# A hybrid attention and RWKV-7 layer on one core: accumulator banks, early pieces, compression weights, the y transposes and the corner products changed together

## The chip, the core and the metric

The kernel runs on one core of a Trainium2 chip. Its time is device time in microseconds (us) of one execution; several executions were timed, and the median counts. Engines are named as in the profile: PE is the matmul engine TensorE (PEld its weight loads), DVE is VectorE, ACT is ScalarE, POOL is GpSimd, and SP is the queue that issues nearly all DMAs.

## What is computed

One decoder layer over 256 tokens of width 2048, in float32: a pre-norm, one combined input projection, two groups of heads that read its columns, an output projection, a post-norm and the residual.

```
hn = rms_norm(h, pre_norm_g)
proj = hn @ w_in
q, kv6, gates, z_a, feat_b, z_b = split(proj)
o_a = nsa_mixer(q, k_cmp, v_cmp, k_slc, v_slc, k_win, v_win, gates, ...)   # 8 heads of 128
o_b = rwkv7_mixer(feat_b, ...)                                             # 16 heads of 64
mix = concat([o_a * silu(z_a), o_b * silu(z_b)])
h = h + rms_norm(mix @ w_out, post_norm_g)
```

The attention group compresses its keys and values in blocks of 32 tokens (`silu(flat @ w1) @ w2`, w1 of 4096 x 128 for keys and for values). The RWKV group runs a recurrence over the tokens for each head: the state is decayed, gets a rank-one correction and a rank-one update, and is read out as y; y is normalized per head, scaled, and gets a bonus term.

## The kernel before

**Pieces.** All products with w_in and w_out are made from float32r parts: a weight tile is cast to a high part H (ACT, L287) and a low part L (DVE, L288), x likewise (xH, xL), and H·xH + H·xL + L·xH is accumulated. The input projection is cut into feature-major pieces of 128 columns (the list `FM`), each in two halves of 24 matmuls of 128x256 (`half_piece`, L379), so piece 27 consists of the halves 270 and 271, and their tiles are called hf270 and lf270. After piece 36 come the token-major pieces (`token_major`, L1118): two windows w, each of six parts (ht00 to ht05, ht10 to ht15), that give values and gates with tokens on the partitions. The output projection has four column blocks n of eight weight parts j each (ho04 is n = 0, j = 4), 12 matmuls of 128x512 to a part.

**Accumulators.** PSUM has eight banks. Two belong to `ppool`, for pieces; six are `banks`, for everything else (L181, L182). The first four pieces (`N_FIRST`) use two of each kind. The next ones up to `N_EARLY` = 6 (L57, L393) also take theirs from `banks`, since no piece can be evacuated before the row statistics of x are known (`row_statistics`, L433, which ends with a copy into `rbc`, L455). In `token_major` both accumulators of a window come from `ppool` (L1121), and ACT evacuates them (L1138, L1139).

**Chains beside the pieces.** Generators run between pieces: they emit a step, yield an estimated time, and go on when the kernel's own clock (`now`, advanced by each matmul) has passed it. The lanes are the RWKV blocks, `solve` (L713) for each half of the RWKV heads, two lanes for attention heads, `compress` (L924) and the gates. Scratch tiles come from an arena of 51 units. The instructions so emitted have priorities by class (chain before evacuation before RWKV before attention before pieces), and a scheduler that assumes a duration for each instruction lays out the final order of every engine. On the chip each engine keeps that order and waits where an operand is late.

**`solve`.** It sends the 32x32 triangular corners of GR through DRAM (L724, L730), inverts them in 31 steps on DVE (L737, L739), stores the inverses and their transposes (zs, zt, L745, L746), loads them back (L759, L766), makes the off-diagonal corner products on PE (L775, L793), and then runs four chunks: G = GR·VS (+ AR·state), the correction with ZB, the state update, and y (L871, L876), which ACT copies out (L878). After the loop it squares y (L888), sums (L889), takes a root (L892) and a reciprocal, scales y (L894), transposes it by head pairs (L903) and adds it into `mix[1]` (L904). `gate_b` (L1108) applies the gate and splits the result into mixB (L1105, L1106), which the parts j = 4 to 7 of the output projection read. The second half's `solve` starts after the first half's loop is over.

**`compress`.** For keys, then for values, it needs w1 in four loads of 512 KB. It keeps one load ahead (L943, L947), and each load is tied to the last or last but one finished half-piece (`pace`).

Of the kernel before, what the change touches and what calls it, by code (L numbers as in the profile page):

```python
# [14 lines left out]
ALU = mybir.AluOpType  # L15

P = 128
T = 256
# [28 lines left out]
V_MU, V_G, V_W0, V_A0, V_KK, V_KA, V_RK, V_LNW, V_LNB = 0, 25, 41, 49, 57, 65, 73, 81, 89  # L47
# [6 lines left out]

N_FIRST = 4

N_EARLY = 6  # L57

NA = 3

# [10 lines left out]

ZLAT = 1.0
GLAT = 1.5

NL = 2

# [43 lines left out]
def hybrid_block(ctx: ExitStack, tc: tile.TileContext, xT, xtok, wfm, wtm, wout, vecs, gpost, lora, table,  # L120
                 onehot, consts, pos, cw1, cw2, out):
    nc = tc.nc
    PE, DVE, ACT, POOL, SP = nc.tensor, nc.vector, nc.scalar, nc.gpsimd, nc.sync
# [34 lines left out]
    def pace(ins, to=None):  # L158


        tc.add_manual_dep(ins.ins, (to or last[0]).ins.name,
                          mybir.DependencyInfo(mybir.DependencyClass.Sync, mybir.DependencyReason.DATA),
                          reason="pace")

    def transpose(o, i, idn):
        now[0] += 0.11
        PE.transpose(out=o, in_=i, identity=idn)  # L167
# [11 lines left out]
    arena = Pool(lambda a, k: arena_[:, a * T:(a + k) * T], UNITS, now)  # L179
    banks_ = ps.tile([P, 8, 512], F32, name="banks")  # L180
    banks = Pool(lambda a, k: banks_[:, NPP + a, :] if k == 1 else banks_[:, NPP + a:NPP + a + k, :], 8 - NPP, now)  # L181
    ppool = Pool(lambda a, k: banks_[:, a, :], NPP, now)  # L182

    def sb(k=1):
        while arena.find(k) is None:
            yield lambda: arena.find(k) is not None
        return arena.take(k)
# [60 lines left out]
    def pick(pool, k, step_=1):  # L248
        until(lambda: pool.find(k, step_) is not None)
        return pool.take(k, step_)  # L250

    def vcol(base, m):
        return vec[:, base + m:base + m + 1]
# [138 lines left out]
    first = deque(pick(ppool if j < NPP else banks, 1) for j in range(N_FIRST))  # L392
    early = deque(pick(banks, 1) for j in range(N_FIRST, N_EARLY))  # L393
    marks = []
# [24 lines left out]
    ident = cst[:, K_ID:K_ID + P]  # L419
# [73 lines left out]
    mix, asked = [None, None], [False, False]  # L493
# [219 lines left out]
    def solve(hb):  # L713
# [49 lines left out]
        for par in range(2):  # L763
            b0 = 64 * (1 - par)
            for a in range(2):
                SP.dma_start(ZT[b0:b0 + 32, :, a, :], ztv[0, par, :, :, a])  # L766
        yield 9.0
        t2p = yield from bank2()
        t2v = t2p[:, :, 0:T].rearrange("p b (j a s) -> p b j a s", j=4, a=2)
        for i in range(4):  # L770
            for hh in range(2):
                for c in range(4):
                    b0 = 64 * (1 - c % 2)
                    q0 = 64 * (i % 2) + 32
# [12 lines left out]
        for i in range(4):  # L787
            for hh in range(2):
                for c in range(4):
                    q = 2 * (i // 2) + hh  # L790
                    j = 4 * q + c
                    q0 = 64 * (i % 2)
# [11 lines left out]
        ysb = ysbs.ap  # L804
        SB, SC, SBo = None, None, None
        for c in range(4):
# [3 lines left out]
            for i in range(4):  # L810
                q0 = 64 * (i % 2)
# [5 lines left out]
            if c:  # L817
                for i in range(4):
                    q0 = 64 * (i % 2)
# [8 lines left out]
            for i in range(4):  # L828
                q0 = 64 * (i % 2)
                for hh in range(2):  # L830
                    o = (i // 2) * P + 64 * hh
# [62 lines left out]
        DVE.tensor_tensor(ysb.rearrange("p (g v) -> p g v", g=16), ysb.rearrange("p (g v) -> p g v", g=16),  # L894
                          rn[:, :, None].to_broadcast([P, 16, 64]), op=ALU.mult)
        yield 2.0
        for i in range(4):
            m = 4 * hb + i
            q0 = 64 * (i % 2)
            ytp = yield from bank()  # L900
            for c in range(4):
                o = T * c + P * (i // 2)
                transpose(ytp[:, 64 * c:64 * c + 64], ysb[q0:q0 + 64, o:o + P], ident[q0:q0 + 64, q0:q0 + 64])  # L903
            DVE.scalar_tensor_tensor(mix[1][:, m, :], ytp[:, :T], vcol(V_LNW, m), mix[1][:, m, :], op0=ALU.mult,  # L904
                                     op1=ALU.add)
            ytp.free(2.0)
            yield 0.5
        ysbs.free(1.0)
# [12 lines left out]
    ready_kv = {"kc": False, "vc": False, "tm": False}  # L921
    POOL.memset(vcS.bitcast(F32), 0.0)

    def compress(a, nm):  # L924
        if a == 0:
            pace(SP.dma_start(post, pos), marks[-2])
            pace(SP.dma_start(w2t, cw2), marks[-2])
        blks = yield from sb(4)
        blk = blks.ap.rearrange("p (j g i) -> p j g i", j=32, g=2)
        POOL.memset(blk[:, :, :, 15:16], 0.0)  # L930
        src = cT[nm].ap
        for g in range(2):
            w_g = bass.AP(tensor=src.tensor, offset=src.offset + g * T, ap=[src.ap[0], [1, 32], [16, 15]])
            DVE.tensor_tensor(blk[:, :, g, 0:15], w_g, post[:, a, :, None].to_broadcast([P, 32, 15]), op=ALU.add)
        cT[nm].free(2.0)
        yield 1.0
        cps = yield from bank()
        w1n = None
        for hf in range(4):
            w1 = w1n  # L940
            if w1 is None:
                w1 = yield from sb(4)
                pace(SP.dma_start(w1[:], cw1[a, :, 8 * hf:8 * hf + 8, :].rearrange("p j d -> p (j d)")), marks[-2])  # L943
                yield 3.0
            if hf < 3:
                w1n = yield from sb(4)
                pace(SP.dma_start(w1n[:], cw1[a, :, 8 * hf + 8:8 * hf + 16, :].rearrange("p j d -> p (j d)")),  # L947
                     marks[-1])
            for j in range(2):
                for q in range(4):  # L950
                    jj = 4 * j + q
                    mm(cps[32 * q:32 * q + 32, 0:P], blk[:, 8 * hf + jj].rearrange("p g i -> p (g i)"),
                       w1[:, jj * P:jj * P + P], start=hf == 0 and j == 0, stop=hf == 3 and j == 1)
            w1.free(1.0)
            yield 2.0
        blks.free(1.0)
        csb = yield from sb()
        DVE.tensor_copy(csb[:, 0:P], cps[:, 0:P])
        cps.free(1.0)
        yps = yield from bank()  # L960
        mm(yps[:, 0:32], csb[:, 0:P], qsum, start=True, stop=True)
        csb.free(1.0)
        yh = tp.tile([P, 32], F32, tag="yh", name=f"yh{nm}")
        DVE.tensor_scalar(yh, yps[:, 0:32], 0.5, None, op0=ALU.mult)
        yps.free(1.0)
        yt = tp.tile([P, 32], F32, tag="yt", name=f"yt{nm}")
        ACT.activation(yt, yh, AF.Tanh)
        DVE.scalar_tensor_tensor(yh, yt, 1.0, yh, op0=ALU.add, op1=ALU.mult)
        yield 2.0
        ops = yield from bank()  # L970
        if a == 0:
            mm(ops[:, 0:32], w2t[:, a, :], yh, start=True, stop=True)
            for g in range(2):
                ACT.activation(KCH[:, g, 128:144], ops[:, 16 * g:16 * g + 16], AF.Copy)
                DVE.tensor_tensor(KCL[:, g, 128:144], ops[:, 16 * g:16 * g + 16], KCH[:, g, 128:144].bitcast(F32),
                                  op=ALU.subtract)
        else:
            for g in range(2):
                mm(ops[0:16, g * P:(g + 1) * P], yh[:, 16 * g:16 * g + 16], w2t[:, a, :], start=True, stop=True)
            opv = ops[0:16, 0:2 * P].rearrange("p (g d) -> p g d", g=2)  # L980
            ACT.activation(vcS[0:16], opv, AF.Copy)
            ACT.activation(vcS[64:80], opv, AF.Copy)
            DVE.tensor_tensor(vcS[32:48], opv, vcS[0:16].bitcast(F32), op=ALU.subtract)
        ops.free(2.0)
        ready_kv[nm] = True
        yield 0.4
# [131 lines left out]
    def token_major():  # L1118
        VV = N_.VV = pick(arena, 4).ap.rearrange("p (w i t) -> p w i t", w=2, i=2)
        for w in range(2):  # L1120
            pts = [pick(ppool, 1) for i in range(2)]  # L1121
            for hf in range(len(TMK) - 1):
                H, L = take()
                with at("proj"):
                    for part in range(2):
                        for k in range(TMK[hf + 1] - TMK[hf]):
                            kk_ = TMK[hf] + k
                            for i in range(2):
                                xs = slice(i * P, (i + 1) * P)
                                if part == 0:  # L1130
                                    mm(pts[i][:, 0:268], xH[:, kk_, xs], H[:, k, :], start=kk_ == 0, stop=False)
                                    mm(pts[i][:, 0:268], xL[:, kk_, xs], H[:, k, :], start=False, stop=False)
                                else:
                                    mm(pts[i][:, 0:268], xH[:, kk_, xs], L[:, k, :], start=False, stop=kk_ == NK - 1)
                progress()
            with at("evac"):
                for i in range(2):
                    ACT.activation(VV[:, w, i, :], pts[i][:, 0:T], AF.Copy, scale=rst[:, i:i + 1])  # L1138
                    ACT.activation(gate[:, i, 12 * w:12 * w + 12], pts[i][:, T:268], AF.Tanh, scale=rsth[:, i:i + 1])  # L1139
                    pts[i].free(1.0)  # L1140
        DVE.tensor_scalar(gate, gate, 0.5, 0.5, op0=ALU.mult, op1=ALU.add)
        ready_kv["tm"] = True
# [6 lines left out]
    for j, (nm, i) in enumerate(FM):  # L1149
# [27 lines left out]
        elif nm in ("r", "v"):  # L1177
            o = pick(arena, 1)
# [66 lines left out]
    for n in range(NA):  # L1245
        pts = out_part(n, range(4), ppool if n % 2 == 0 else banks)
# [51 lines left out]
    for n in range(4):  # L1298
# [7 lines left out]
        pts = out_part(n, js, ppool if n % 2 == 0 else banks, order)  # L1306
# [85 lines left out]
```

## Time and profile before

| | |
|---|---|
| time, median of 3 runs (lowest to highest) | 577.52 us (576.17 to 577.62) |
| the profiled execution | 575.76 us, of which the program's span is 574.0 us |
| PE busy | 557.3 us (97%), 4812 matmuls |
| PEld busy | 519.4 us |
| DVE busy | 426.7 us (74%) |
| ACT busy | 311.8 us |
| POOL busy | 55.8 us |
| DMA | 99.97 MB, mean 174 GB/s |
| granted TensorE clock, mean over the span | 0.996 of full speed |

Busy time on PE is the union of its matmuls. Idle time of an engine that nothing waits for costs nothing, so the list of what PE waited for is the view to read with it. Times in the trace count from the start of the span.

### The profile page before, as it was taken

How to read it: one execution, taken by the hardware profiler on the slowest of the kernel's cores; microseconds unless marked ns; L12 is line 12 of the kernel's file. 1: busy time of each engine (PE TensorE's matmuls, PEld its weight loads, DVE VectorE, ACT ScalarE, POOL GpSimd, SP SyncE). 2: the span in 40 equal slices, each digit the busy share in tenths (PEclk: the TensorE clock that was granted, in tenths of full speed). 3: DMA queues.
4: the chain of work that ended last, by engine and by line, in shares of the span. 5: the costliest groups of instructions: out<-in, count | busy, mean ns of one | idle time of the engine just before them, and what ended most of it. 6: DMA issues, size and time to landing. Idle time of an engine off the chain costs nothing.

```text
span 574.0 us, 12180 instructions
## 1 busy us (share of the span) xinstructions
PE 557.3 (97%) x4812; PEld 519.4 (90%) x4812; DVE 426.7 (74%) x892; ACT 311.8 (54%) x566; POOL 55.8 (10%) x95
## 2 busy tenths in 40 slices
PE   9999999999999999999999999999999999999994
PEld 8998999998989999999988999999999987777883
DVE  5888997867988666569789369899766473576855
ACT  6858764623445434457675468566633353564632
POOL 3202300400000000141031000000000000000002
PEclk9999999999999999999999999999999999999998
DMA  8967444557675844333346253356634455674723
GB/s 293 367 199 248 148 163 140 189 156 237 215 268 154 214 145 148 121 114 104 99 138 212 95 156 120 120 167 209 186 114 146 136 158 188 185 293 153 227 90 147
DMA packets 41365, 99.97 MB, mean 174 GB/s; under 512 B 14395, under 2 KB 17116, under 8 KB 40924
## 3 DMA queue, kind: packets, MB, share of 16 engines
q1 hardware_dynamic: 41020, 98.88, 53.2%
q8 instruction: 38, 0.62, 0.5%
q10 hardware_dynamic: 288, 0.31, 0.2%
q14 instruction: 19, 0.16, 0.1%
HBM read 93.93 MB, written 5.24 MB: 173 GB/s over the span
## 4 chain that ended last, share of the span: by engine, by line
PE 78%; DMA 7%; DVE 5%; ACT 4%; issue 2%; SPq 1%; POOL 1%; DVEq 0%; ACTq 0%
PE banks L154 76%; PE banks L167 2%; DMA arena<-in_cw_dram 2%; DMA us<-GR 1%; DMA arena<-us 1%; DMA rf__96<-in_wfm_dram 1%; DMA rf__2334<-in_wfm_dram 1%; DMA zs<-arena 1%; DMA arena<-zt 1%; DVE y L1289 0%; SPq L724 0%; DVE small L537 0%; ACT arena L1036 0%; ACT L892 0%; POOL arena L627 0%
## 5 line engine op out<-in xcount | busy, mean ns | idle before, releaser
L154 PE MATMUL banks<-arena 128*32 128x128 f32 (+3 forms) x470 | 32.3, 255 | 2.1 <-POOL arena L269 1.1
L154 PEld LDWEIGHTS banks<-arena 128*32 128x32 f32 (+3 forms) x470 | 26.6, 137 | 5.7 <-DMA arena<-in_cw_dram 1.5
L737 DVE TENSOR_TENSOR arena<-arena 64x31 f32<-64x31 f32 (+15 forms) x62 | 20.5, 330 | 8.0 <-DMA arena<-us 7.3
L539 ACT ACTIVATE small<-small 128x256 f32<-128x256 f32 x25 | 12.4, 503 | 17.2 <-DVE small L537 17.1
L739 DVE TENSOR_TENSOR arena<-arena 64x31 f32<-64x31 f32 (+15 forms) x62 | 20.4, 330 | 0.8
L167 PE MATMUL banks<-small,arena 128*128 128x128 f32 (+1 forms) x112 | 16.8, 263 | 0.1
L1094 ACT ACTIVATE arena<-arena 128x256 f32<-128x256 f32 x16 | 6.6, 415 | 18.2 <-DVE arena L1208 15.0
L154 PE MATMUL banks<-AR,arena 64*128 64x128 f32 x128 | 15.4, 289 | 0.0
L154 PEld LDWEIGHTS banks<-AR,arena 64*128 64x128 f32 x128 | 12.2, 187 | 2.4 <-issue 0.5
L167 PEld LDWEIGHTS banks<-small,arena 128*128 128x128 f32 (+1 forms) x112 | 11.8, 139 | 2.6 <-issue 1.1
L594 DVE RECIPROCAL arena<-arena 128x256 f32<-128x256 f32 x8 | 13.8, 1739 | 0.4 <-ACT arena L591 0.2
L1036 ACT ACTIVATE arena<-arena,mx 128x128 f32<-128x128 f32 (+1 forms) x32 | 14.1, 442 | 0.0
L627 POOL TENSOR_SCALAR arena<-arena,small 128x256 f32<-128x256 f32 x8 | 9.8, 1220 | 42.7 <-DVE small L537 34.9
L624 POOL TENSOR_SCALAR arena<-arena 128x256 f32<-128x256 f32 x8 | 9.5, 1187 | 38.8 <-ACT arena L623 37.6
L540 DVE SCALAR_TENSOR_TENSOR arena<-small 128x256 f32<-128x256 f32 x25 | 11.8, 481 | 1.9 <-ACT small L539 1.9
L1293 POOL TENSOR_TENSOR y<-y,xres 128x512 f32<-128x512 f32 x2 | 2.9, 1454 | 101.5 <-ACT y L1292 101.5
L154 PE MATMUL banks<-VS,GR 128*64 128x64 f32 x256 | 11.4, 228 | 0.0
L154 PEld LDWEIGHTS banks<-VS,GR 128*64 128x64 f32 x256 | 9.5, 137 | 1.8 <-issue 0.7
L687 DVE TENSOR_TENSOR GR<-banks,small 128x1024 f32<-128x1024 f32 x8 | 9.8, 1221 | 0.9 <-PE banks L154 0.9
L537 DVE TENSOR_TENSOR small<-banks,small 128x256 f32<-128x256 f32 x25 | 10.3, 417 | 0.2
L1032 DVE CUSTOM_DVE_ANT_0 arena<-banks,arena 128x128 f32<-128x128 f32 (+1 forms) x32 | 10.1, 348 | 0.0
L864 POOL TENSOR_TENSOR arena<-arena,PC 128x256 f32<-128x256 f32 x4 | 2.7, 685 | 71.5 <-DVE arena L854 36.3
(1375 smaller groups left out, 2143.4 us busy)
## 6 DMA issues: line engine op xcount, KB each, us to landing
arena<-in_cw_dram SPq DMA_DIRECT2D x8, 512.0 KB, 4.7
arena<-in_wfm_dram SPq DMA_DIRECT2D x4, 512.0 KB, 8.9
xres<-in_xtok_dram SPq DMA_DIRECT2D x2, 1024.0 KB, 7.5
xr<-in_xT_dram SPq DMA_DIRECT2D x3, 512.0 KB, 7.2
bscr<-arena SPq DMA_DIRECT2D x1, 1536.0 KB
out_dram<-y SPq DMA_DIRECT2D x5, 256.0 KB, 2.3
arena<-bscr SPq DMA_DIRECT2D x8, 128.0 KB, 3.2
gpt<-in_gpost_dram SPq DMA_DIRECT2D x1, 1024.0 KB, 5.0
```

Source lines behind the costliest of these rows:

```text
L154: last[0] = PE.matmul(o, lhsT, rhs, **kw)
L167: PE.transpose(out=o, in_=i, identity=idn)
L537: DVE.tensor_tensor(f[:, 1:T + 1], pt[:, :T], rbc, op=ALU.mult)
L539: ACT.activation(tm, f[:, 0:T], AF.Copy, scale=vcol(V_MU, c))
L540: DVE.scalar_tensor_tensor(o, f[:, 1:T + 1], omu[:, c:c + 1], tm, op0=ALU.mult, op1=ALU.add)
L594: pace(DVE.reciprocal(A.nrm[i + j], A.nrm[i + j]))
L627: POOL.tensor_scalar(fk[:], ta[:], ka2[:, m:m + 1], ka1[:, m:m + 1], op0=ALU.mult, op1=ALU.add)
L687: DVE.tensor_tensor(A.GR[:, i].rearrange("p h c t -> p (h c) t"), gp.ap.rearrange("p h (c t) -> p (h c) t", c=4), gmask[:, None, :].to_bro ...
L737: DVE.tensor_tensor(t_, U[:, 0:j, j:j + 1].to_broadcast([64, j, w]), Z[:, j:j + 1, j:32].to_broadcast([64, j, w]), op=ALU.mult)
L739: DVE.tensor_tensor(Z[:, 0:j, j:32], Z[:, 0:j, j:32], t_, op=ALU.add)
L1032: DVE.tensor_tensor_reduce(out=dst, in0=src, in1=bb, scale=1.0, scalar=-3.0e38, op0=ALU.add, op1=ALU.max, accum_out=mx[:, i, j:j + 1])
L1036: ACT.activation(dst, dst, AF.Exp, bias=mx[:, i, j:j + 1], accum_out=sm[:, i, j:j + 1])
```

## The change

Five edits. `token_major` takes one accumulator of each window from `ppool` and one from `banks`. `N_EARLY` is 7. The compression weights are fetched by `fetch_cw` up to two parts ahead of the one in use, from a common count of eight parts for keys and values, as long as the arena has room (at least 12 free units, unless the part is needed at once). The corner products stand 11 instead of 9 us after the loads that they need. The final transposes of y take 128 partitions at a time, so that a half has 8 of 128x128 instead of 16 of 64 partitions, in two banks instead of four, and DVE reads the two halves of each bank by a strided view.

```diff
-N_EARLY = 6
+N_EARLY = 7
+CWLAT = 2.5
@@ solve
-        yield 9.0
+        yield 11.0
         t2p = yield from bank2()
@@
-        for i in range(4):
-            m = 4 * hb + i
-            q0 = 64 * (i % 2)
+        for a in range(2):
             ytp = yield from bank()
             for c in range(4):
-                o = T * c + P * (i // 2)
-                transpose(ytp[:, 64 * c:64 * c + 64], ysb[q0:q0 + 64, o:o + P], ident[q0:q0 + 64, q0:q0 + 64])
-            DVE.scalar_tensor_tensor(mix[1][:, m, :], ytp[:, :T], vcol(V_LNW, m), mix[1][:, m, :], op0=ALU.mult,
-                                     op1=ALU.add)
+                o = T * c + P * a
+                transpose(ytp[:, P * c:P * c + P], ysb[:, o:o + P], ident)
+            ytv = ytp.ap.rearrange("p (c b t) -> p c b t", c=4, b=2)
+            for b in range(2):
+                m = 4 * hb + 2 * a + b
+                mv = mix[1][:, m, :].rearrange("p (c t) -> p c t", c=4)
+                DVE.scalar_tensor_tensor(mv, ytv[:, :, b, :], vcol(V_LNW, m), mv, op0=ALU.mult, op1=ALU.add)
             ytp.free(2.0)
             yield 0.5
@@ compress
+    cws, cwn = {}, [0]
+    def fetch_cw(upto, must):
+        while cwn[0] < upto and arena.find(4) is not None and (must or arena.busy.count(False) >= 12):
+            n = cwn[0]
+            cws[n] = arena.take(4)
+            cwn[0] += 1
+            pace(SP.dma_start(cws[n][:], cw1[n // 4, :, 8 * (n % 4):8 * (n % 4) + 8, :].rearrange("p j d -> p (j d)")),
+                 marks[-2])
     def compress(a, nm):
         if a == 0:
             pace(SP.dma_start(post, pos), marks[-2])
             pace(SP.dma_start(w2t, cw2), marks[-2])
+            fetch_cw(2, False)
@@
-        w1n = None
         for hf in range(4):
-            w1 = w1n
-            if w1 is None:
-                w1 = yield from sb(4)
-                pace(SP.dma_start(w1[:], cw1[a, :, 8 * hf:8 * hf + 8, :].rearrange("p j d -> p (j d)")), marks[-2])
-                yield 3.0
-            if hf < 3:
-                w1n = yield from sb(4)
-                pace(SP.dma_start(w1n[:], cw1[a, :, 8 * hf + 8:8 * hf + 16, :].rearrange("p j d -> p (j d)")),
-                     marks[-1])
+            n = 4 * a + hf
+            fetch_cw(min(n + 3, 8), False)
+            if n not in cws:
+                yield lambda: arena.find(4) is not None
+                fetch_cw(n + 1, True)
+                yield 4.0
+            w1 = cws.pop(n)
@@
             w1.free(1.0)
-            yield 2.0
+            yield CWLAT
@@ token_major
-            pts = [pick(ppool, 1) for i in range(2)]
+            pts = [pick(pool, 1) for pool in (ppool, banks)]
```

The scheduler lays the program out anew. Three places on PE, each before and then after the change (lines of the changed kernel are two or more higher).

First, PE where the first token-major window ends (ht05, lt05) and the second begins (ht10). KCH, KCL, qh1 and ql1 belong to an attention head's logits, hr and bonr to sums of an RWKV block. Before:

```order
L154 MATMUL banks_74<-lt05__3267,xH_76 128x268 x4
L154 MATMUL banks_74<-KCH_296,qh1_3718 128x256
L154 MATMUL banks_74<-KCH_296,ql1_3719 128x256
L154 MATMUL banks_74<-KCL_297,qh1_3718 128x256
L154 MATMUL banks_74<-ht10__3305,xH_76 128x268
L154 MATMUL banks_74<-ht10__3305,xL_75 128x268
```

After:

```order
L156 MATMUL banks_74<-hr22_3382,bonr_284 128x256
L156 MATMUL banks_74<-hr23_3383,bonr_284 128x256
L156 MATMUL banks_74<-ht05__3259,xL_75 128x268
L156 MATMUL banks_74<-ht10__3292,xH_76 128x268
L156 MATMUL banks_74<-ht10__3292,xL_75 128x268
L156 MATMUL banks_74<-ht10__3292,xH_76 128x268
L156 MATMUL banks_74<-lt05__3258,xH_76 128x268 x4
```

Matmuls of the second window now stand between those of the first; before, all of them stood behind it and behind three products of a head.

Second, PE where the row statistics end: the 128x256 product with `small` spreads the row factors (it feeds `rbc`), the 128x384 one makes the bias rows of `bias_rows`. Before:

```order
L154 MATMUL banks_74<-xH_76,lf51__475 128x256 x8
L154 MATMUL banks_74<-arena_73,small_72 128x256
L154 MATMUL banks_74<-arena_73,small_72 128x384
L154 MATMUL banks_74<-xH_76,hf60__506 128x256
L154 MATMUL banks_74<-xL_75,hf60__506 128x256
```

After:

```order
L156 MATMUL banks_74<-xH_76,hf60__506 128x256
L156 MATMUL banks_74<-xL_75,hf60__506 128x256
L156 MATMUL banks_74<-arena_73,small_72 128x256
L156 MATMUL banks_74<-xH_76,hf60__506 128x256
L156 MATMUL banks_74<-xL_75,hf60__506 128x256
```

Piece 6 now begins before the 128x256 product, and the 128x384 one stands 24 matmuls of that piece behind it instead of next to it.

Third, PE at the end of the second half's `solve`: VS1, GR1 and AR1 are the last y product, 128x64 and 128x128 with `small` the y transposes, ho and lo the output projection. Before, 42 matmuls of 128x512 stand between the last y product and the first transposes; these are the last of them:

```order
L154 MATMUL banks_74<-ho23__6033,mixA_5769 128x512 x4
L154 MATMUL banks_74<-lo23__6032,mixA_5769 128x512 x2
L154 MATMUL banks_74<-ho04__6059,mixB_6000 128x512 x4
L154 MATMUL banks_74<-lo04__6058,mixB_6000 128x512 x2
L154 MATMUL banks_74<-ho05__6085,mixB_6000 128x512 x4
L154 MATMUL banks_74<-lo05__6084,mixB_6000 128x512 x2
L167 MATMUL banks_74<-small_72,arena_73 128x64 x4
L154 MATMUL banks_74<-ho04__6059,mixB_6000 128x512 x4
```

After, from the last y product on:

```order
L156 MATMUL banks_74<-arena_73,AR1_3346 64x128 x4
L156 MATMUL banks_74<-ho04__6043,mixB_6010 128x512 x7
L156 MATMUL banks_74<-lo04__6042,mixB_6010 128x512 x2
L156 MATMUL banks_74<-ho04__6043,mixB_6010 128x512
L156 MATMUL banks_74<-lo04__6042,mixB_6010 128x512 x2
L156 MATMUL banks_74<-ho05__6070,mixB_6010 128x512 x7
L156 MATMUL banks_74<-lo05__6069,mixB_6010 128x512 x2
L156 MATMUL banks_74<-ho05__6070,mixB_6010 128x512
L156 MATMUL banks_74<-lo05__6069,mixB_6010 128x512 x2
L156 MATMUL banks_74<-ho14__6155,mixB_6010 128x512 x4
L169 MATMUL banks_74<-small_72,arena_73 128x128 x4
L156 MATMUL banks_74<-lo14__6154,mixB_6010 128x512 x2
```

28 matmuls instead of 42 stand between the y product and the transposes, and the first of them reads mixB, which is split only after that y product has released GR.

## Rows read from the trace of the kernel before

**Rows 1.** The profile's page, its first lines: span, and busy time of the engines.

```profile
span 574.0 us, 12180 instructions
PE 557.3 (97%) x4812; PEld 519.4 (90%) x4812; DVE 426.7 (74%) x892; ACT 311.8 (54%) x566; POOL 55.8 (10%) x95
```

**Rows 2.** Busy time by stretch; columns: stretch, length, each engine's busy time, clock, DMA.

```profile
8.30:565.80 557.50, 550.25 (x4777) 512.67 (x4777) 418.62 (x875) 305.02 (x553) 51.13 (x78) 1.00 0.54 173
307.70:407.30 99.60, 97.70 (x783) 95.32 (x784) 82.30 (x303) 63.33 (x164) 4.84 (x12) 1.00 0.48 149
360.00:380.00 20.00, 20.00 (x167) 19.89 (x166) 18.27 (x59) 11.19 (x28) 0.23 (x1) 1.00 0.44 139
380.00:400.00 20.00, 20.00 (x166) 19.84 (x165) 18.67 (x64) 13.50 (x33) 0.23 (x1) 1.00 0.58 181
```

**Rows 3.** What PE waited for: us in total, times, longest us.

```profile
PE banks L154 <- ACT small L1139: 2.5, 2, 1.4
PE banks L154 <- DVE small L455: 1.2, 1, 1.2
...
PE banks L154 <- DMA arena<-in_cw_dram: 1.0, 1, 1.0
PE banks L154 <- DMA arena<-zt: 0.7, 1, 0.7
PE banks L154 <- DVE arena L1208: 0.7, 1, 0.7
PE banks L167 <- DVE lcs L1050: 0.6, 1, 0.6
```

**Rows 4.** The chain that ended last, two stretches of matmuls: start, length, how many.

```profile
8.28 34.31 PE banks L154 x283
...
521.49 44.29 PE banks L154 x194
```

**Rows 5.** PE in order of time: transposes of 64 partitions, then of 128.

```profile
510.93 0.61 PE L154 MATMUL banks<-lo__6084,mixB 128*128 128x512 f32 x2
511.48 0.46 PE L167 MATMUL banks<-small,arena 64*128 64x64 f32 x4
511.87 1.20 PE L154 MATMUL banks<-ho__6059,mixB 128*128 128x512 f32 x4
...
86.21 0.60 PE L167 MATMUL banks<-small,arena 128*128 128x128 f32 x4
86.57 0.36 PE L154 MATMUL banks<-xH,hf__991 128*128 128x256 f32 x1
```

**Rows 6.** PE, ACT and DVE in order of time, from the last y product to its scaling.

```profile
500.75 0.66 PE L154 MATMUL banks<-arena,AR 128*64 128x128 f32 x8
502.57 1.06 ACT L287 ACTIVATE ho__6085<-ro__6082 128x1024 fp32r<-128x1024 f32 x1
503.53 1.04 ACT L888 ACTIVATE arena<-arena 128x1024 f32<-128x1024 f32 x1
508.30 1.23 DVE L894 TENSOR_TENSOR arena<-arena,small 128x1024 f32<-128x1024 f32 x1
509.44 1.22 DVE L288 TENSOR_TENSOR lo__6107<-ro__6105,ho__6108 128x1024 fp32r<-128x1024 f32 x1
```

**Rows 7.** Single lines on DVE: how often, then shortest, median and longest in ns.

```profile
L1032 DVE DVE_READ_ACCUMULATOR2_ANT mx<- x48: 71/81/90, 280.7 to 402.6; 128x1 f32 x48
L1032 DVE CUSTOM_DVE_ANT_0 arena<-banks,arena x32: 273/350/425, 280.7 to 402.3; 128x128 f32<-128x128 f32 x16, 128x256 f32<-128x256 f32 x16
L687 DVE TENSOR_TENSOR GR<-banks,small x8: 1214/1222/1225, 81.2 to 330.7; 128x1024 f32<-128x1024 f32 x8
L629 DVE TENSOR_TENSOR_SCAN arena<-small,arena x8: 676/680/693, 57.8 to 291.9; 128x256 f32<-128x256 f32 x8
L653 DVE TENSOR_TENSOR arena<-arena x8: 411/417/426, 69.6 to 309.5; 128x256 f32<-128x256 f32 x8
L1044 DVE RECIPROCAL sm<-sm x16: 159/166/179, 285.2 to 406.9; 128x3 f32<-128x3 f32 x16
```

## The prediction

> **What bounds the kernel now.** I read the page's first lines, then busy time by stretch, then the list of what PE waited for, and only then single instructions. The reader is to see in the first lines that PE is busy 557.3 of 574.0 us [rows 1]. The rest of the span lies mostly at its ends: from 8.30 to 565.80 us PE is busy 550.25 of 557.50 us [rows 2]. So a change can win in two ways alone. It can take away some of those 7.25 us of waiting, or it can take matmul time away. The list of waits says what the 7.25 us are: two waits for ACT's evacuation of the token-major pieces, 2.5 us; one for the copy of the row factors on DVE (L455), 1.2 us; one for compression weights, 1.0 us; one for the corner inverses (zt), 0.7 us; and two of 0.7 and 0.6 us that no edit aims at [rows 3]. Inside its stretches PE runs at an even pace: 283 matmuls in 34.31 us, nearly all of 256 columns, are 0.121 us each, and 194 of 512 columns in 44.29 us are 0.228 us each [rows 4]. A half-piece of 24 matmuls is therefore 2.9 us.
>
> All terms are taken against the profiled execution, 575.76 us with a span of 574.0. It is 1.76 us below the median of 577.52, and I carry every difference over to the median unchanged.
>
> **Token-major pieces.** Removed is the need of the second window for both banks of the first, and of piece 37 for a bank of the second window, since the first window's `ppool` bank is free by then. Both waits of 2.5 us in total hang on that [rows 3]. The new order bears it out: matmuls of ht10 now stand between those of ht05. The gain lies between 0 (something else is late there) and 2.5; I take 2.5, since the wait is for a bank and the bank is another one. What it adds is that chains have one bank of six less for some 30 us. That delays generators, not pieces, and comes back below as a later chain.
>
> **Seven early pieces.** The 1.2 us wait stands before the 128x384 product for the bias rows and ends with the copy L455 of the row statistics [rows 3]. PE had nothing else to do: pieces 0 to 5 held their banks, and none can be evacuated before that copy. In the new order 24 matmuls of piece 6, 24 x 0.121 = 2.9 us, stand between. That is more than 1.2 us, so the whole 1.2 goes; its bounds are 0 and 1.2.
>
> **Compression weights.** Eight loads of 512 KB remain eight, on the same queue. In the new order of SP the third and fourth load stand ahead of the solve's four corner stores instead of behind them, so I take the 1.0 us as gone [rows 3]; bounds 0 (it returns at another part) and 1.0. In return, the solve's reload of its corners stands behind one more weight load on SP's queue. With the bank lost to the token-major pieces and the changed order of DVE, the first half's corner products move from the second half of piece 27 to the first half of piece 30, five half-pieces or 14 us. Nobody on PE waits for them there; what is late next is the second half's chain, priced below.
>
> **Later corner products.** The wait for zt is 0.7 us [rows 3]. The yield shifts when the generator emits, but chain work has a high priority, and the final order is laid out by assumed durations. The products stand 3.6 half-pieces' worth of weights behind the last zt load instead of 3.8. So I take 0.3, between 0 and 0.7.
>
> **y transposes.** Before, a group of four 64-partition transposes holds PE from 511.48 to 511.87, 0.39 us, and the two matmuls ahead of it end their share at 510.93 + 2 x 0.228 = 511.39, so with the 0.09 us gap a group costs 0.48 us [rows 4, 5]. Four 128-partition transposes cost 86.57 - 86.21 = 0.36 us and have no such gap [rows 5]. Eight groups become four: without the gap 8 x 0.39 - 4 x 0.36 = 1.7 us, with it 8 x 0.48 - 4 x 0.36 = 2.4 us. I take 2.1. The eight additions on DVE stay eight of the same size.
>
> These rows show the four transposes of a group one after the other, and all four read the same 64 partitions. [...]
>
> **The tail, which the change exposes.** After the last y product the chain goes through ACT and DVE: it ended at 500.75 + 0.66 = 501.41, and the scaling L894 ended at 508.30 + 1.23 = 509.53, so 8.1 us [rows 6]. Before, 42 matmuls, 42 x 0.228 = 9.6 us, covered that. Now 28 do, 6.4 us. In the new order of ACT the cast of ho05 (1.06 us, between the y copy and the square [rows 6]) has gone ahead of the chain, so the chain should take 8.1 - 1.06 = 7.1 us: PE waits 0.7 us, or 1.7 if the chain keeps its 8.1. Behind L894 stands the cast of lo14 on DVE, 1.2 us [rows 6], and PE reads lo14 right after the first four transposes (0.36 us): another 0.8 us. The first part on mixB now follows the last y product at once, while one split on ACT and one on DVE, some 0.4 us each as the 256-column line has it [rows 7], must come between, and the last products on AR cover 0.66 us of it [rows 6]: 0.2 us. Two DVE additions ahead of the next split add 0.3. Sum 2.0 us; bounds 0 (if chains come earlier on the chip than their places suggest) and 3.0.
>
> **What stays unknown.** A new order from assumed durations will have waits of its own. Before, those that no edit touches were 0.7 + 0.6 = 1.3 us [rows 3]; they may go or come again. I charge the same amount once more, 1.3, with bounds 0 and 3.
>
> **Sum.** 2.5 + 1.2 + 1.0 + 0.3 + 2.1 = 7.1 us gained, 2.0 + 1.3 = 3.3 us lost, so -3.8 us: 572.0 in the frame of the profiled execution, 573.7 us as a median. The best ends give -(2.5 + 1.2 + 1.0 + 0.7 + 2.4) = -7.8, 569.7 us.
>
> **Rivals.** *The waits only move* (A). The scheduler knew none of these waits either. If half of the 5.0 us of gained waits (2.5 + 1.2 + 1.0 + 0.3) returns elsewhere, and the tail costs its 3.0 with 1.3 beside it, the sum is -(2.5 + 2.1) + 3.0 + 1.3 = -0.3: 577.2 us. For it speaks that the waits came from late ACT, DVE and DMA work, which is still there; against it, that two of the edits give PE another bank rather than better timing.
>
> *VectorE becomes the bound* (B). Between the casts of pieces 38 and 50 DVE was busy 82.30 of 99.60 us, 83%, and PE was nearly full [rows 2]. The later chain moves work into this stretch: counting the new order, 12 logits additions of 0.350 us and 12 readouts of 0.081, 2 masks of 1.222, 2 scans of 0.680, 12 operations of 0.16 on three columns and 12 of 0.417 on 256 columns, together 16.0 us [rows 7]. DVE then has 98.3 us of work; PE has some 23 small matmuls more, 2.8 us, so 102.4 us. The best DVE share in the trace is 18.27 + 18.67 of 40 us, 92% [rows 2]. At that share it needs 106.4 us, and the three L tiles cast ahead, 3 x 2.9 = 8.7 us, cover the difference. If it only keeps 83%, it needs 119.0 us and PE loses 119.0 - 102.4 - 8.7 = 7.9 us: 573.7 + 7.9 = 581.6 us, slower than before. The point from which this decides is a share of 84%: there the loss is 5.5 us, the 3.8 gained and 1.7 more.
>
> [...]
>
> **How the numbers follow.** Forecast 0.60, A 0.20, B 0.14, C 0.06. A measurement of this kernel can tell about 0.3% (1.7 us) from no change, so faster means below 575.8 and slower above 579.3. Faster: 0.56 of the forecast, 0.04 of A, 0.03 of C, together 0.63. Same: 0.04 of the forecast, 0.15 of A, 0.03 of C, together 0.22. Slower: nearly all of B and a little of A, 0.15. The range reaches from the best ends, 569.7, over A and C to 580.0; left out are most of B and the rare case that even the unknown waits turn out a gain, under 0.2 together.
>
> **What would show it.** In the changed profile the list of what PE waited for should have no ACT L1139-like wait (its line is now L1152) and no wait for the row-factor copy; the count of matmuls falls by 16; four 128-partition transposes follow each other at 0.36 us. Near the last transposes there should be new idle time of about 2 us, behind the scaling of y and behind lo14. PE's idle time between its first and last stretch should be near 5 us instead of 7.25. The prediction is wrong if that idle time is not below 7, if PE shows waits for casts (L lines) between 320 and 420 us, or if matmul time itself changes by more than the transposes do.

## The result, and the profile after

The changed kernel takes 571.43 us as a median (569.78 to 572.31), the kernel before 577.48 (576.17 to 577.62) beside it: a ratio of 0.9897, 95% interval 0.987 to 0.9924. That is 6.05 us less by the medians; between the two profiled executions it is 575.76 - 571.67 = 4.1 us. Forecast were 3.8. Of all executions compared below, one of run e5's eight (1360 us) was in the slow state and is left out. The first lines of the page after, to be held against [rows 1]:

```profile
span 569.9 us, 12187 instructions
PE 552.9 (97%) x4796; PEld 519.1 (91%) x4796; DVE 427.1 (75%) x892; ACT 311.1 (55%) x566; POOL 56.3 (10%) x95
```

PE has 16 matmuls fewer, as said, but 4.4 us less matmul time, where the sum had 2.1. Busy time by stretch (length, PE, PEld, DVE, ACT, POOL, granted clock, DMA, GB/s), the first row from the start of the even stretch to the last product:

```profile
8.30:561.70 553.40, 546.62 (x4763) 513.21 (x4761) 419.25 (x876) 304.73 (x554) 51.58 (x78) 0.99 0.54 174
210.00:215.00 5.00, 2.21 (x63) 1.72 (x64) 1.40 (x2) 0.68 (x2) 0.00 (x0) 0.76 0.94 261
215.00:220.00 5.00, 5.00 (x46) 4.94 (x35) 3.23 (x6) 1.06 (x1) 0.00 (x0) 0.56 0.05 19
```

PE idles 553.40 - 546.62 = 6.78 us there, against 7.25 before [rows 2] and the 5 that I expected; in a second profile of the same kernel (e13 below) it is 8.27 us. So the waits gained almost nothing; what they are made of has changed, though. What PE waited for after (us in total, times, longest):

```profile
PE banks L156 <- DMA arena<-zt: 2.8, 1, 2.8
PE banks L156 <- DMA arena<-in_cw_dram: 1.8, 2, 1.5
...
PE banks L156 <- ACT xH L360: 0.9, 1, 0.9
PE banks L169 <- DVE arena L656: 0.5, 1, 0.5
PE banks L156 <- DVE lo__6154 L290: 0.5, 1, 0.5
PE banks L156 <- ACT mixB L1118: 0.4, 1, 0.4
...
PE banks L169 <- DVE arena L896: 0.2, 1, 0.2
```

The token-major wait (2.5 us) and the row-factor wait (1.2) of [rows 3] are gone. The wait for compression weights has grown from 1.0 to 1.8 us, that for zt from 0.7 to 2.8, and the three kinds at the tail (lo14, mixB, the scaling of y), together 1.1 us, are new, as are the waits for xH (0.9) at the start and for L656 (0.5).

Behind the zt wait stands the low clock of the stretches above. SP and PE in order of time (start, length, engine, line, and in brackets the idle time before and what ended it):

```profile
202.54 1.81 SPq L761 DMA_DIRECT2D arena<-zs  x4
...
204.89 1.92 SPq L761 DMA_DIRECT2D arena<-zs  x4
207.40 0.35 SPq L281 DMA_DIRECT2D rf__2582<-in_wfm_dram  x1
207.80 1.91 SPq L768 DMA_DIRECT2D arena<-zt  x4
```

```profile
210.06 0.28 PE L156 MATMUL banks<-xL,hf__2436 128*128 128x256 f32 x1
210.18 0.28 PE L156 MATMUL banks<-xH,hf__2436 128*128 128x256 f32 x1
213.25 0.31 PE L156 MATMUL banks<-arena,GR 32*32 32x32 f32 x2 [2.79 <-DMA arena<-zt]
214.00 1.39 PE L156 MATMUL banks<-arena,GR 32*32 32x32 f32 x62
...
216.12 0.41 PE L156 MATMUL banks<-xL,hf__2436 128*128 128x256 f32 x1
216.33 0.41 PE L156 MATMUL banks<-xH,hf__2436 128*128 128x256 f32 x1
```

The four zt loads were issued from 207.80 to 209.71 us, and their products were due at 210.4. Behind the wait the same matmuls of 256 columns come every 0.21 us instead of 0.12: 18 of them take the 4.0 us from 215.31 to 219.32, where 18 x 0.121 would be 2.2.

The tail, PE from the last y product to the transposes, and the scaling of y on DVE, to be held against [rows 5, 6]:

```profile
503.81 0.66 PE L156 MATMUL banks<-arena,AR 128*64 128x128 f32 x8
504.85 1.90 PE L156 MATMUL banks<-ho__6043,mixB 128*128 128x512 f32 x7 [0.38 <-ACT mixB L1118]
...
511.74 0.66 PE L169 MATMUL banks<-small,arena 128*128 128x128 f32 x4 [0.24 <-DVE arena L896]
512.88 0.73 PE L156 MATMUL banks<-lo__6154,mixB 128*128 128x512 f32 x2 [0.48 <-DVE lo__6154 L290]
...
514.38 0.60 PE L169 MATMUL banks<-small,arena 128*128 128x128 f32 x4
514.73 1.64 PE L156 MATMUL banks<-ho__6097,mixB 128*128 128x512 f32 x6
```

```profile
510.46 1.22 DVE L896 TENSOR_TENSOR arena<-arena,small 128x1024 f32<-128x1024 f32 x1
```

From the end of the y product (504.47) to the end of the scaling (511.68) are 7.2 us, where 7.1 were forecast, and PE waits at the three places named. The second group of transposes takes 514.73 - 514.38 = 0.35 us.

### The profile page after: what moved, and what is told of

The parts are those of the page before. It is cut to its first block, busy times and chain, and to the rows that moved or that the text cites. A ratio compares the mean times of both kernels' runs of the same rounds, so it can differ in the third digit from the quotient of the medians.

```text
span 569.9 us, 12187 instructions
## 1 busy us (share of the span) xinstructions
PE 552.9 (97%) x4796; PEld 519.1 (91%) x4796; DVE 427.1 (75%) x892; ACT 311.1 (55%) x566; POOL 56.3 (10%) x95
## 4 chain that ended last, share of the span: by engine, by line
PE 86%; DMA 5%; DVE 4%; ACT 2%; issue 1%; POOL 1%; SPq 1%; DVEq 0%; ACTq 0%; POOLq 0%
PE banks L156 84%; PE banks L169 2%; DMA arena<-zt 1%; DMA arena<-in_cw_dram 1%; DMA arena<-us 1%; DMA us<-GR 1%; DMA xr<-in_xT_dram 1%; POOL arena L629 1%; DVE y L1302 0%; DMA arena<-zs 0%; DVE arena L950 0%; SPq L726 0%; DVE arena L739 0%; DVE arena L631 0%; POOL arena L630 0%
## 5 line engine op out<-in xcount | busy, mean ns | idle before, releaser
L156 PE MATMUL banks<-arena 128*32 128x128 f32 (+3 forms) x470 | 30.4, 252 | 2.9 <-DMA arena<-in_cw_dram 1.8
L169 PE MATMUL banks<-small,arena 128*128 128x128 f32 x96 | 15.8, 275 | 0.8 <-DVE arena L656 0.5
L1049 ACT ACTIVATE arena<-arena,mx 128x256 f32<-128x256 f32 (+1 forms) x32 | 14.1, 443 | 0.0
L169 PEld LDWEIGHTS banks<-small,arena 128*128 128x128 f32 x96 | 11.3, 140 | 1.9 <-DVE arena L656 0.7
L539 DVE TENSOR_TENSOR small<-banks,small 128x256 f32<-128x256 f32 x25 | 10.2, 414 | 0.1
L1045 DVE CUSTOM_DVE_ANT_0 arena<-banks,arena 128x256 f32<-128x256 f32 (+1 forms) x32 | 10.1, 348 | 0.0
L862 POOL MEMSET arena<- 64x256 f32 x12 | 3.7, 308 | 64.6 <-DVE arena L1108 36.5
L626 POOL TENSOR_SCALAR arena<-arena 128x256 f32<-128x256 f32 x8 | 8.1, 1013 | 17.6 <-ACT arena L625 17.5
```

The lines of the kernel that those rows point to most:

```text
L156: last[0] = PE.matmul(o, lhsT, rhs, **kw)
L539: DVE.tensor_tensor(f[:, 1:T + 1], pt[:, :T], rbc, op=ALU.mult)
L1045: DVE.tensor_tensor_reduce(out=dst, in0=src, in1=bb, scale=1.0, scalar=-3.0e38, op0=ALU.add, op1=ALU.max, accum_out=mx[:, i, j:j + 1])
L1049: ACT.activation(dst, dst, AF.Exp, bias=mx[:, i, j:j + 1], accum_out=sm[:, i, j:j + 1])
```

## The experiments

Two theories went into these runs. By the bank theory the terms of the sum are properties of the edits, so each goes and comes with its edit. By its rival, the order theory, each edit makes the scheduler lay another order, and that order's own waits are as large as the terms. The ratio is to the kernel before on the same chip. "Idle" is PE's idle time between its first and last matmul, "busy" its matmul time, both of the one profiled execution; the last column holds the 5 us stretches (from 0 on) before the last product with a granted clock under 0.98. In these terms the kernel before has 7.4 us of idle and no such stretch, the changed one 7.7 and two (0.76, 0.56).

| run | median us | ratio (95%) | idle, busy us | low clock |
|---|---|---|---|---|
| e1 changed, token-major as before | 575.51 | 0.998 (0.9963 to 0.9997) | 10.6, 553.8 | 0.78, 0.88 |
| e2 changed, 6 early pieces | 572.37 | 0.9916 (0.989 to 0.9942) | 6.3, 555.3 | 0.71, 0.94 |
| e3 changed, weights as before | 569.04 | 0.987 (0.984 to 0.99) | 2.8, 553.4 | none |
| e4 changed, y transposes as before | 583.66 | 1.0113 (1.0076 to 1.015) | 13.5, 560.3 | six, 0.50 to 0.90 |
| e5 before, y transposes alone | 573.73 | 0.9949 (0.9932 to 0.9966) | 7.2, 554.6 | 0.66 |
| e6 before, 7 early pieces alone | 580.41 | 1.0063 (1.0043 to 1.0083) | 11.6, 557.7 | 0.66 |
| e7 before, token-major alone | 573.92 | 0.9971 (0.9947 to 0.9995) | 6.3, 556.6 | none |
| e11 changed, corner products pushed back | 574.18 | 0.9969 (0.9951 to 0.9987) | 9.2, 554.0 | 0.66 |
| e8 changed, corner yield 9.0 as before | 567.03 | 0.9828 (0.9813 to 0.9842) | 3.6, 552.4 | none |
| e9 changed, zt loads first | 572.62 | 0.9933 (0.9911 to 0.9956) | 7.1, 557.3 | 0.91, 0.75, 0.63, 0.69 |
| e14 e3 once more | 569.50 | 0.9889 (0.9862 to 0.9916) | 4.5, 553.6 | none |
| e13 changed, once more | 571.43 | 0.9898 (0.988 to 0.9915) | 8.5, 552.8 | 0.66 |

**Token-major pieces: e1 and e7.** In e1 one line of the changed kernel is put back; e7 is the kernel before with that line alone changed.

```diff
-            pts = [pick(pool, 1) for pool in (ppool, banks)]
+            pts = [pick(ppool, 1) for i in range(2)]
```

> The changed kernel with both accumulators of a token-major window from the piece banks again. If the gain is the sum of the waits removed (bank theory), the two waits on the evacuation return: 2.5 us, so about 573.9 us. If each new layout simply brings its own waits and its own number of switches between kinds of matmuls (order theory), the difference from 571.4 has no relation to 2.5 us, and other waits of 1 to 3 us appear or go elsewhere, above all the one on the transposed corner inverses.

> The kernel before with token-major accumulators of both kinds alone. Bank theory: 2.5 us less, 575.0 us. Order theory: no relation to 2.5 us.

In e1 the wait is back, larger than before, and the clock falls to 0.78 and 0.88 in the stretches at and behind it:

```profile
PE banks L156 <- ACT small L1152: 4.0, 1, 4.0
```

In e7 no wait of that line is left, and the kernel is faster by 0.29%. The wait belongs to the bank, as forecast. Its price does not: 0.83% of the ratio (4.8 us) in the changed layout, 1.7 us in the old one.

**Early pieces: e2 and e6.** One constant, in the changed kernel and in the one before.

```diff
 e2
-N_EARLY = 7
+N_EARLY = 6
 e6
-N_EARLY = 6
+N_EARLY = 7
```

> The changed kernel with 6 early pieces instead of 7. Bank theory: the 1.2 us wait at the copy of the row factors returns, about 572.6 us. Order theory: a difference without relation to 1.2 us.

> The kernel before with 7 early pieces alone. Bank theory: 1.2 us less, 576.3 us, and the wait for the copy of the row factors gone. Order theory: no relation to 1.2 us.

In e2 the row-factor wait is back with its 1.2 us:

```profile
PE banks L156 <- DVE small L457: 1.2, 1, 1.2
```

Yet the zt wait is absent from e2's list, and the intervals of e2 and of the changed kernel overlap. In e6 the row-factor wait is gone, and the kernel is slower by 0.63%: its list has 3.3 us for weights, 1.7 for L1055 and 1.0 for L623 instead, which no early piece touches. Of the two theories only the order theory allows that.

**Compression weights: e3 and e14.** The third edit is taken out; e14 is the same program again, beside the changed kernel (e13).

```diff
-            fetch_cw(min(n + 3, 8), False)
...
-            w1 = cws.pop(n)
+            w1 = w1n
...
+                w1n = yield from sb(4)
+                pace(SP.dma_start(w1n[:], cw1[...]), marks[-1])
...
-            yield CWLAT
+            yield 2.0
```

> The changed kernel with the compression weights fetched one part ahead as before. In the changed kernel the wait for these weights is 1.8 us, before it was 1.0 us. Bank theory: the prefetch itself gave nothing, so the time stays within 1 us of 571.4 us or falls by 0.8 us. My prediction had counted 1.0 us for it: then 572.4 us. Order theory: the wait on the transposed corner inverses (2.8 us and the halved clock behind it) changes with it.

> The changed kernel with the compression weights loaded one part ahead, as before; the same program as the earlier run of that name, taken again beside the changed kernel on one chip. If the prefetch two parts ahead is what costs the 1.8 us wait for weights and the later zt wait, this one is again faster than the changed kernel by about 2.4 us (568.5 to 570 us, with 3 us of TensorE waits in the profile and no stretch of lowered clock before the last product); if the earlier difference was chance, the two agree within 1 us.

> The changed kernel itself once more, as the other half of that comparison: 570.5 to 572.5 us, with the zt wait of about 2.8 us at 211 us and the granted clock below 0.8 behind it.

By its ratio the first is faster than the changed kernel by 0.27% (1.6 us), the second by 0.09% (0.5 us), and in both cases the intervals overlap. Over all executions of both programs (12 and 10) the means differ by 1.5 us, plus or minus 1.3, but they come from different chips, on which the means of the kernel before itself lie up to 0.7 us apart. So no gain from the prefetch shows here, and whether it cost a little is open. What it was to remove isn't a fixed thing either: one program's wait for weights was 1.0 us in e3's profile and 2.6 in e14's.

**y transposes: e4 and e5.** The block of the last transposes is put back in e4, and is the only one changed in e5 (the same diff with its signs turned).

```diff
-                transpose(ytp[:, P * c:P * c + P], ysb[:, o:o + P], ident)
+                transpose(ytp[:, 64 * c:64 * c + 64], ysb[q0:q0 + 64, o:o + P], ident[q0:q0 + 64, q0:q0 + 64])
```

> The changed kernel with the old y transposes, 16 of 64 partitions to a half. Bank theory: 2.1 us of matmul time returns, about 573.5 us; the last transposes come earlier or later by less than 1 us. Order theory: no relation to 2.1 us. [...]

> The kernel before with the new y transposes alone. Bank theory: 2.1 us less matmul time, 577.5 - 2.1 = 575.4 us, all waits of before kept. Order theory: anything, with waits that differ from those of before.

Alone the edit gives 0.51%, 2.9 us. Taking it out of the changed kernel costs 2.2%, six times the 2.1 us that its instructions were priced at. Of the 13.2 us more in e4's span, 5.8 are waits and 7.4 matmul time. One of its waits, and stretches behind two of the long ones (the zt wait, 2.2 us, at 213 us and the one for L1066 at 382):

```profile
PE banks L169 <- ACT arena L1066: 1.9, 1, 1.9
```

```profile
215.00:220.00 5.00, 5.00 (x65) 4.94 (x59) 2.90 (x6) 1.06 (x1) 0.00 (x0) 0.50 0.21 86
380.00:385.00 5.00, 3.13 (x21) 2.66 (x20) 5.00 (x20) 3.85 (x11) 0.00 (x0) 0.90 0.81 265
385.00:390.00 5.00, 5.00 (x36) 5.00 (x35) 3.57 (x12) 2.43 (x5) 0.23 (x1) 0.76 0.14 54
```

The transposes have nothing to do with a head's L1066 at 380 us, where DVE is busy 5.00 of 5.00 us. It is the order around them that is another.

**Corner products: e11, e9, e8.** The zt wait of 2.8 us was the largest new cost. e11 ties the first 32 corner products to the last but one finished half-piece, so that they stand later on PE, e9 issues the four zt loads ahead of the eight zs loads, and e8 undoes the edit. The edit was not made alone in the kernel before, and neither was the prefetch.

```diff
 e11
                     mm(t2v[...], ...)
+                    pace(last[0], marks[-2])
 e9
-        for mp in range(2): ... SP.dma_start(ZBv[...], zsv[...])
         for par in range(2): ... SP.dma_start(ZT[...], ztv[...])
+        for mp in range(2): ... SP.dma_start(ZBv[...], zsv[...])
 e8
-        yield 11.0
+        yield 9.0
```

> The changed kernel with the corner products tied behind the last but one finished piece, so that they stand 39 matmuls (4.7 us) later on PE, behind piece 30. If the wait for the transposed inverses costs what the trace shows, its 2.8 us go and so does the halved clock behind it, which stretched some 5 us of matmuls by 2 to 3 us: 571.4 - 5 = 566.4 us. Rival: the chain of the half comes about 2 us later for it, and the tail behind the last y product gives that back: 571.4 - 5 + 2 = 568.4 us. If the clock's fall in the trace costs nothing, 568.6 us.

> The changed kernel with the four corner loads that the first corner products read issued ahead of the other corner loads on SyncE's queue. Load theory: the 2.79 us wait for zt falls below 1 us, the granted clock stays at 1.00 at 210 to 220 us, and the time falls by 2 us of wait and up to 2.4 us of clock: 567 to 570 us. Order theory: the products now stand elsewhere in the order, other waits take the place of this one (as in the run that held them back behind piece 30), and the time stays within 2 us of the changed kernel's: 570 to 574 us.

> The changed kernel with the corner products two half-pieces earlier, as before (9.0 for 11.0). Bank theory: the wait for a corner stood at 0.5 to 0.7 us before, so that undoing this edit costs 0.3 us and no more: 571.3 to 572.3 us, and all other waits stay where they are. Order theory: the whole order after piece 30 is laid anew, so that the time may move by 3 us either way; what sets it is whether a wait of 2 us or more stands in front of TensorE anywhere, since the runs so far show the granted clock falling behind each such wait but one (0.56 to 0.9 for 5 us): 568 to 575 us, and the profile's long waits tell on which side.

e11 removes the wait for zt and is slower than the changed kernel; its list begins with two waits that this edit doesn't touch:

```profile
PE banks L156 <- ACT arena L1083: 2.1, 1, 2.1
...
PE banks L156 <- ACT cTt L1082: 1.0, 1, 1.0
```

e9 has the loads 3 us sooner, from 204.73 us on, but its scheduler puts the products sooner as well; they wait 0.72 and 1.41 us, and the clock falls all the same, to 0.63 and 0.69. e8 is the fastest of all. Its interval lies clear of the changed kernel's beside it (0.9813 to 0.9842 against 0.988 to 0.9915), 4.4 us below it and 10.2 below the kernel before. So it beats both. What PE waited for in it, beside 1.1 us at the start and 0.5 us in all behind two lines of DVE (no wait for zt among it):

```profile
PE banks L156 <- DMA arena<-in_cw_dram: 1.6, 2, 1.1
...
PE banks L156 <- DVE arena L1221: 0.7, 1, 0.7
PE banks L156 <- ACT mixA L1118: 0.5, 1, 0.5
```

Its corner loads and products, SP and then PE:

```profile
205.45 0.45 SPq L768 DMA_DIRECT2D arena<-zt  x1
206.00 0.39 SPq L281 DMA_DIRECT2D rf__2582<-in_wfm_dram  x1
206.43 1.42 SPq L768 DMA_DIRECT2D arena<-zt  x3
```

```profile
208.03 0.52 PE L156 MATMUL banks<-xH,lf__2403 128*128 128x256 f32 x3
208.48 0.24 PE L156 MATMUL banks<-arena,GR 32*32 32x32 f32 x2
208.65 0.86 PE L156 MATMUL banks<-xH,lf__2403 128*128 128x256 f32 x5
...
210.75 0.92 PE L156 MATMUL banks<-arena,GR 32*32 32x32 f32 x62
```

The bulk of the products runs at the same place as in the changed kernel (210.75 us, there due at 210.4), but the last loads are issued 1.9 us sooner (the rows end at 207.85 and 209.71), with a weight load less ahead of the first. And the second half's chain is further ahead: in the two profiles its last y product ends at 494.29 and 504.47 us, and its transposes begin 10.0 us behind it in e8 and 7.3 in the changed kernel. The tail's waits are gone with that:

```profile
493.63 0.66 PE L156 MATMUL banks<-arena,AR 128*64 128x128 f32 x8
...
504.30 0.60 PE L169 MATMUL banks<-small,arena 128*128 128x128 f32 x4
504.65 1.17 PE L156 MATMUL banks<-ho__6052,mixB 128*128 128x512 f32 x4
```

## Why the prediction was right, and where its steps were not

The time was in the range and the direction was the likeliest one; by medians the gain was 6.05 us instead of 3.8. But the sum met the result through errors that cancel, and as far as the parts go that is luck.

- **Token-major, 2.5 us: right** as a wait (e1, e7). As a part of the time it was worth 1.7 us alone and 4.8 in the changed layout.
- **Early pieces, 1.2 us: right as a wait, wrong as a part.** The wait goes with the edit in both directions (e2, e6), but alone the edit costs 0.63%.
- **Compression weights, 1.0 us: not gained.** The wait went to 1.8 us. The step that failed is "I take the 1.0 us as gone": it read a gain from the loads' places on SP. No run here shows a gain from the edit.
- **Later corner products, 0.3 us: not gained, and the largest error.** The wait grew by 2.1 us, with a clock of 0.56 behind it, and undoing the edit gains 4.4 us. The edit does not make that wait by itself: e2 keeps it and has no wait for zt, e3 and e14 keep it with 0.7 us. The step that failed is that "the products stand 3.6 half-pieces' worth of weights behind the last zt load", some 10 us. In the trace the last load was issued 209.71 - 210.4, that is 0.7 us, before the products were due: SP issued nothing between 200.1 and 202.5 us, until the zs store of the solve had landed (issued at 197.46, 5.0 us), then needed some 0.47 us for each of twelve corner loads, and the first zt load, issued at 207.80, took 5.4 us to land. A distance counted in weight loads on SP isn't a distance in time on PE. "Nobody on PE waits for them there" fell with it.
- **y transposes, 2.1 us: right in size.** In e5 the 64-partition transposes' share of PE's time (from one start to the next, idle taken off) of 3.10 us is replaced by 1.70 us more for those of 128, and the 512-column products around them lose 0.75 us with the gaps: 2.15. A group of 128 took 0.35 us, one of 64 partitions 0.39 [rows 5]. Rival C, to which the chances give 0.06, has this term at nothing. No run here shows that: e5 shows the 2.15 us, so C is out.
- **The tail, 2.0 us: right in its places, too large.** 0.38 for the split on mixB (0.2), 0.24 for the scaling (0.7), 0.48 for lo14 (0.8), nothing for the additions (0.3): 1.1 us. e8 and e3 show it isn't a price of the wider transposes: where the chain is ahead, PE waits for none of these.
- **Unknown waits, 1.3 us: too small.** The two old ones of 0.7 and 0.6 us are gone, and new ones are the zt and weight waits above, 0.9 for xH at the start and 0.5 for L656. Across the runs PE's idle time moved between 2.8 and 13.5 us. That, not 0 to 3, was the spread to allow for. Nor had the sum a term for the clock.
- **Matmul time: wrong.** It fell by 4.4 us, more than the transposes do, in spite of the clock of 0.76 and 0.56 from 210 to 220 us. That is the last of the prediction's own signs of being wrong. Two groups of matmuls on PE (count, then busy us and mean ns), before, after, and in e13, which is the changed kernel once more:

```profile
L154 PE MATMUL banks<-arena 128*128 128x128 f32 x54 | 11.2, 337 | 1.1 <-POOL arena L269 1.1
...
L154 PE MATMUL banks<-hr,bonr 128*128 128x256 f32 x32 | 9.3, 316 | 0.2 <-ACT hr L572 0.2
```

```profile
L156 PE MATMUL banks<-arena 128*128 128x128 f32 x54 | 10.4, 316 | 1.1 <-POOL arena L271 1.1
L156 PE MATMUL banks<-hr,bonr 128*128 128x256 f32 x32 | 8.6, 299 | 0.0
```

```profile
L156 PE MATMUL banks<-arena 128*128 128x128 f32 x54 | 11.2, 336 | 1.1 <-POOL arena L271 1.1
...
L156 PE MATMUL banks<-hr,bonr 128*128 128x256 f32 x32 | 8.6, 300 | 0.0
```

The 0.7 us of the second group, whose instructions are the same in number and shape, goes with the new order. The 0.8 us of the first does not: in e13, with the same order, it is back at 11.2 us. Nor are the two groups less broken up by other products: on PE they stand in 17 and 26 runs of their own kind, before in 17 and 27. The rest of the 4.4 us is spread over many groups. Why matmul time fell by more than the transposes is open; no run varied that alone.

Rival A (the waits only move) was right about the idle time, 6.78 us (8.27 in e13) after 7.25: the first of the signs, idle time not below 7, is just missed in one profile and met in the other. It was wrong about the total only because matmul time fell. Rival B (VectorE) isn't seen: between 320 and 420 us PE is busy 99.81 of 100 us in the changed profile, DVE 85.72, past the 84% from which it was to decide. In e4 its place does show up, with 1.9, 1.0 and 1.0 us of waits for heads between 380 and 405 us.

Shown, then: that the token-major wait and the row-factor wait go with their edits, both ways, that the transposes are worth their price alone, and that the sizes of the parts depend on the layout. The three edits that were made alone (e5, e6, e7) sum to 0.17% less time, the five together give 1.03%. Of the bank theory only the two waits and the transposes' price stood. Left open is why the scheduler's order is good in e8 and e3 and bad in e4 and e6; the runs show only by which waits.

## What to carry to other kernels

Where a scheduler lays the whole program anew, price an edit's own wait from the trace, but allow for the layout as a term of its own: here it was worth several us either way, in most runs more than the edit's own term. Undo each edit of a bundle by itself before keeping it; in this bundle one of the five cost 4.4 us, and without it the other four are 1.7% faster than the kernel before. A load's distance to its reader is to be taken as the time from issue to the moment that the reader is due, with the stores and the issues on its queue that lie between.

## What was not expected of the hardware

**A wait of PE can cost twice.** Behind the 2.79 us wait for zt in the changed kernel, the 18 matmuls from 215.31 us on take 4.0 us instead of 2.2, another 1.8. In the kernel before and in e3, e7, e8 and e14 the longest wait was 1.6 us or less and no stretch of 5 us before the last product had a granted clock under 0.98. In the changed kernel, e1, e2, e4, e6 and e11, waits of 1.9 to 4.0 us each lay in or before stretches of 0.50 to 0.94. The lowest, 0.50, is e4's from 215 to 220 us, and the changed kernel has 0.50 in each microsecond from 213 to 219. Length alone doesn't tell: the wait for the row factors of 1.22 us was followed by 0.66 in e5 and by 1.00 in the kernel before, with the same work around it; a wait for weights of 1.87 us at 151 us in e13 was followed by 1.00; and in e9 the clock fell behind a wait of 0.51 us at 116 us, which the changed kernel has too, without a fall. The stretch of e5, then that wait and the stretch behind it in e9, and the same stretch in the changed kernel:

```profile
45.00:50.00 5.00, 5.00 (x31) 5.00 (x31) 3.32 (x8) 4.86 (x10) 0.00 (x0) 0.66 0.91 340
...
116.33 0.55 PE L169 MATMUL banks<-small,arena 128*128 128x128 f32 x3 [0.51 <-DVE arena L656]
120.00:125.00 5.00, 5.00 (x35) 4.49 (x37) 1.60 (x3) 1.06 (x1) 0.51 (x2) 0.75 0.44 167
...
120.00:125.00 5.00, 5.00 (x62) 4.29 (x61) 2.82 (x3) 1.06 (x1) 0.76 (x2) 1.00 0.68 218
```

So the runs do not show what decides it. In the stretch of e5 PE finished 31 matmuls, and 42 in the same stretch of the kernel before. At the 0.121 us of [rows 4] that is 11 x 0.121 = 1.3 us, as much as the wait itself.

**Two small products inside a run of large ones are dear.** In e8's rows above three products of 256 columns start at 208.03, so the next would start at 208.39; with two of 32x32 between them it starts at 208.65, 0.26 us for the two. The other 62 in one go take 210.75 to 211.60, 0.014 us each.

**Small loads can land late.** The four zt loads of 32 KB of the first half land 4.4 to 5.4 us after their issue in the changed kernel and, as far as the trace has them, 3.3 to 3.9 in e8; those of the second half 2.6 to 3.1 and 1.7 to 2.4. Between SP's corner loads of the first half stand weight loads of 512 KB in both; whether these delay them is not shown, since no run varied it.
